# Ten seven-product quads per sweep in place of eight, the first weight sum of each made in DRAM by an accumulating DMA

## The chip, the cores and the metric

One NeuronCore of one Trainium2 chip runs the whole program. The metric is device time in microseconds (us) of one execution; the median of three runs of the kernel before is 1942.89 us.

The engines are named as the profile names them: PE multiplies matrices (PEld is its weight load, which overlaps), DVE is the vector engine, ACT the scalar engine, POOL is GpSimd, and SP issues most of the DMAs. Each engine runs its own list of instructions in order and waits on semaphores. The DMAs of SP, ACT and POOL are carried by the core's 16 DMA engines.

## The reference

Two layers on a sequence of 256 tokens with 2048 channels, in float32. Layer 0 mixes tokens with a convolution module, layer 1 with latent attention; each is followed by an MLP of width 8192.

```python
for layer in range(2):
    h = rms_norm(x, norm_mixer_g[layer])
    x = x + (conv_module(h, ...) if layer == 0 else mla(h, ...))
    h = rms_norm(x, norm_mlp_g[layer])
    x = x + jnp.square(jax.nn.relu(h @ mlp_w1[layer])) @ mlp_w2[layer]
return rms_norm(x, final_norm_g)
```

The convolution module multiplies by a 2048x4096 matrix (`conv_w_pw1`), gates, applies a causal depthwise convolution of width 31, normalizes, and multiplies by a 2048x2048 matrix.

## The kernel before

**Products in three parts.** Every float32 operand is split into a rounded part `hi` (ACT, one copy) and the rest `lo` (a subtraction, `lo = raw - hi`); a product is then three matmuls, hi by hi, lo by hi and hi by lo (`mm3`, L202 to L204). So each weight block costs a DMA into `raw` (three buffers), one pass of ACT and one pass of DVE or POOL (L169 and L173, or L431 and L432 in a quad), into six `hi` and six `lo` buffers of up to 128x1024.

**The convolution stage** runs over 16 chunks of 128 channels. The weights of one chunk come in two loads, and their four `lo` passes are made by POOL (L173 on POOL), which also multiplies the gate (L815) and adds a half sum (L872). DVE applies the taps of the depthwise convolution (L875), PE multiplies (L788).

**The MLP** takes the hidden width in two halves of 4096, so there are four halves in the program. Of each half, the up product makes eight groups `g` of 512 hidden channels (L645, L646; the activations are in `xt`, sixteen tiles of 128 channels), and squares and splits them (L663 to L673). The down product then makes two sweeps, each over 1024 output columns and all 32 k-tiles of the half, taken by twos: a **plain pair** is 2 k-tiles by 2 column blocks by 2 token blocks, 8 products or 24 matmuls of 512 columns; a **quad** reaches the same result with 7 products, 21 matmuls, from sums of weight blocks and sums of inputs (a Strassen scheme in Winograd's form). Groups 0, 2, 4 and 6 are `mixed` (eight quads per sweep), groups 1, 3, 5 and 7 plain (eight plain pairs). The weight sums of a quad are made by DVE in `raw` (L439, L440, L441), the input sums at the end of the up product of their group (`mixed_inputs`, L459 to L462). Each sweep holds all eight PSUM banks: four for the outputs and four for sums that `join` and `close` add in at the end; in the first half of a layer they are added to `xs` by accumulating DMAs that POOL issues (L512), 24 in the program.

**The order.** The program is written in one sequence, but a scheduler places each engine's instructions by its own estimate of when their inputs are ready; an instruction that waits for nothing can be put far ahead of where it is written. `MIXED`, `HEAD`, `TAIL` and `LAST_TAIL` set where quads stand among the plain pairs: before, a first sweep begins P P q q P q q (P a plain pair, q a quad).

Of the kernel before, what the change touches and what calls it, by code (L numbers as in the profile page):

```python
# [10 lines left out]
F32 = mybir.dt.float32  # L11
# [7 lines left out]
P = 128  # L19
# [23 lines left out]
LOOK = WB // 2 - 1  # L43
MIXED = {(0, 0): (0, 2, 4, 6), (0, 1): (0, 2, 4, 6), (1, 0): (0, 2, 4, 6), (1, 1): (0, 2, 4, 6)}
N_MIXED = 4
HEAD, TAIL, LAST_TAIL = (2, 1), 2, 3

# [31 lines left out]
def trunk_kernel(  # L79
# [31 lines left out]
    wpool = ctx.enter_context(tc.tile_pool(name="wpool", bufs=2))  # L111
    small = ctx.enter_context(tc.tile_pool(name="small", bufs=2))
    psum, psum_cx = {}, [ExitStack()]

# [235 lines left out]
    def open_xt(name):  # L350
        pool = right_pool(name, 1)
        xt[:] = [
            pool.tile([P, KC // NNB, 2 * S], F32R, name=nm("xt")) for _ in range(NNB)
        ]

    xhl = lambda k: xt[k // 4][:, k % 4, :]
    xh = lambda k: xhl(k)[:, :S]
# [65 lines left out]

    def mixed_weights(raw):

        def halves(src):
            hi = wpool.tile(list(src.shape), F32R, tag="hi", name=nm("hi"), bufs=WB)
            lo = wpool.tile(list(src.shape), F32R, tag="lo", name=nm("lo"), bufs=WB)  # L430
            nc.scalar.activation(hi, src, AF.Copy)  # L431
            nc.vector.tensor_tensor(lo, src, hi.bitcast(F32), op=ALU.subtract)  # L432
            return [(hi[:, i, :], lo[:, i, :]) for i in range(src.shape[1])]

        b11, b21 = halves(raw[:, :, :NB])
        (b22,) = halves(raw[:, 1:2, NB:])
        top = raw[:, 0, :].rearrange("p (c n) -> p c n", c=2)
        low = raw[:, 1, :].rearrange("p (c n) -> p c n", c=2)
        nc.vector.tensor_tensor(top, raw[:, :, NB:], top, op=ALU.subtract)  # L439
        nc.vector.tensor_tensor(low[:, 1, :], low[:, 1, :], top[:, 0, :], op=ALU.subtract)  # L440
        nc.vector.tensor_tensor(low[:, 0, :], low[:, 0, :], low[:, 1, :], op=ALU.subtract)  # L441
        t1, t3 = halves(top)
        t4, t2 = halves(low)
        return b11, b21, b22, t1, t2, t3, t4

    def mixed_inputs(v, fh, fl):

        def halves(src, at, n):  # L450
            hi, lo = fh[:, at : at + n, :], fl[:, at : at + n, :]
            nc.scalar.activation(hi, src, AF.Copy)
            nc.vector.tensor_tensor(lo, src, hi.bitcast(F32), op=ALU.subtract)

        a = v.rearrange("p k (t n) -> p (k t) n", t=T)
        a11, a21, a12, a22 = (a[:, i, :] for i in range(4))
        halves(a[:, 0:1, :], 0, 1)
        halves(a[:, 2:4, :], 1, 2)
        nc.vector.tensor_tensor(a22, a21, a22, op=ALU.add)  # L459
        nc.vector.tensor_tensor(a21, a11, a21, op=ALU.subtract)  # L460
        nc.vector.tensor_tensor(a11, a22, a11, op=ALU.subtract)
        nc.vector.tensor_tensor(a12, a12, a11, op=ALU.subtract)  # L462
        halves(a, 3, 4)

    class Sums:
# [13 lines left out]

        def mixed(self, w, k, fh, fl, end):  # L480

            b11, b21, b22, t1, t2, t3, t4 = mixed_weights(load([rows(w, k, 2, self.n * NB, 2 * NB)], 2))
            u1, u6, u7, u5 = self.u
            work = [
                (u1, 0, b11), (u5, 6, t1), (u7, 4, t3), (u6, 3, t2),
                (self.e[0][0], 1, b21), (self.e[0][1], 5, b22), (self.e[1][0], 2, t4),
            ]
            if self.begun:
                work = [work[i] for i in (0, 4, 5, 1, 2, 6, 3)]
            for ps, i, (wh, wl) in work:  # L490
                mm3(ps, fh[:, i, :], fl[:, i, :], wh, wl, self.first(ps), end and any(ps is u for u in self.u))
# [24 lines left out]
        def join(self, room):  # L516
# [6 lines left out]
            nc.vector.tensor_tensor(c, u7, b, op=ALU.add)  # L523
            nc.vector.tensor_tensor(d, u5, c, op=ALU.add)
            nc.vector.tensor_tensor(b, u5, b, op=ALU.add)
            for (t, n), o in (((1, 0), c), ((1, 1), d), ((0, 1), b)):
# [75 lines left out]
    def mlp(layer, ssq, next_gain, finish=None, before=None, between=None, beside=None, after_up=None):  # L602

        with ExitStack() as cx:
# [22 lines left out]
            for hf in range(HALVES):  # L627
                last = hf == HALVES - 1
                mixed = MIXED[layer, hf]
                plain = [g for g in range(ng) if g not in mixed]  # L630
                gs = {}
                for g in range(ng):
                    ps = [acc_tile() for _ in range(4)]
                    c0 = (hf * nkh + 4 * g) * P
                    for u in range(KC // 4):
# [3 lines left out]
                        for j in range(4):  # L639
                            k = 4 * u + j  # L640
                            wh, wl = wj(j)
                            for b in range(4):
# [3 lines left out]
                                nc.tensor.matmul(ps[b][:, :S], wl[:, bs], xh(k), start=False, stop=k == KC - 1)  # L646
                        step(6)
                    if hf == g == 0:
                        scales()
                    if beside is not None and g == 2:  # L650
                        beside(mp)
                        beside = None
                    if g in mixed or g in plain[len(plain) + len(mixed) - N_MIXED :]:
                        shape = [P, 2, 7, P] if g in mixed else [P, 4, S]
                        gs[g] = [mp.tile(shape, F32R, tag=f"s{c}", name=nm(f"s{c}"), bufs=N_MIXED) for c in "hl"]
                    else:
                        gs[g] = [mp.tile([P, 4, S], F32R, tag=f"g{c}", name=nm(f"g{c}"), bufs=ng - N_MIXED) for c in "hl"]
                    gh, gl = gs[g]
# [15 lines left out]
                nssq, add, prepare = residual_stage(last, next_gain)  # L674
                w, k_lo = mlp_w2[layer], hf * nkh
                at_kt = lambda i: lambda k, t: gs[k // 4][i][:, k % 4, t * P : (t + 1) * P]
                hi, lo = at_kt(0), at_kt(1)
                ms = [(g, b) for g in mixed for b in range(2)]
                due = []

                def mixed_quad(sums, i):
                    g, b = ms[i]
                    sums.mixed(w, k_lo + 4 * g + 2 * b, gs[g][0][:, b], gs[g][1][:, b], i == len(ms) - 1)

                split_end = last and finish is not None
                for n in range(0, NNB, 2):
# [5 lines left out]
                    if ends:  # L692
                        after_up()
                    for i, k in enumerate(ks[: -tail] if ends else ks):
                        upto = -(-len(ms) * (i - head + 1) // (len(ks) - head - tail + 1))
                        while at < min(upto, len(ms)):
                            mixed_quad(sums, at)
                            at += 1
                        if i == len(ks) - tail + 1:
                            sums.join(room)  # L700
# [22 lines left out]
    with ExitStack() as cx:  # L723
# [235 lines left out]
        with tc.manual_schedule():  # L959
# [85 lines left out]
            def part(ks, p):  # L1045
                return xt[ks[0] // 4][:, ks[0] % 4 : ks[0] % 4 + len(ks), p * S : (p + 1) * S]

# [744 lines left out]
    with ExitStack():  # L1792
        gfs = []

        def load_gf():
            gfs.append(right_pool("gf", 1).tile([P, D], F32, name="gf"))
            nc.scalar.dma_start(gfs[0], final_norm_g.rearrange("(a n) -> a n", a=1).partition_broadcast(P))
# [90 lines left out]
```

## Time and profile before

| what | value |
|---|---|
| runs | 1942.15, 1942.89, 1943.25 us; median 1942.89 |
| profiled execution | span 1940.9 us from first to last instruction; granted clock 0.998 |
| convolution stage, weights split on POOL | 12 to 197 us of the span |
| up products of the MLP | 300 to 478, 641 to 819, 1246 to 1424, 1587 to 1765 us |
| down products, two sweeps each | 478 to 641, 819 to 985, 1424 to 1587, 1765 to 1931 us |
| DMA | 373.93 MB, mean 193 GB/s |

The profile is of one execution, whose span is 1940.9 us, 2.0 us under the median of the runs. Busy time counts instructions that follow each other closely with their overlap, so an engine that never waits may show a little more than its window. In tables by stretches of time, the number in brackets behind a busy time is that of instructions. A wait is put down to what ended it.

### The profile page before, as it was taken

The numbers are of one execution on the slowest core, as the hardware profiler recorded it, in microseconds if no ns is written. First come the engines' busy times: TensorE is split into PE (matmuls) and PEld (weight loads), VectorE is DVE, ScalarE is ACT, GpSimd is POOL, SyncE is SP. The second block draws the span as 40 slices with busy tenths as digits, with TensorE's granted clock in tenths as the row PEclk, the third lists the DMA queues.
The fourth block names the chain that finished last, engine by engine and source line by source line (L and its number), as shares of the span: only waits on it lengthen the run. The fifth ranks groups of instructions, "written<-read, shape, count | busy, mean of one in ns | idle before, by whom it ended". The sixth has DMA issues, their size and how long they took to land. (4 is left out here: it accounts for less than half of the span.)

```text
span 1940.9 us, 28606 instructions
## 1 busy us (share of the span) xinstructions
PE 1920.0 (99%) x10799; PEld 1683.0 (87%) x10799; DVE 1604.5 (83%) x2490; ACT 1095.4 (56%) x1636; POOL 241.9 (12%) x196
## 2 busy tenths in 40 slices
PE   8999999999999999999999999999999999999997
PEld 8999888888888888888889998888888888888876
DVE  7999988877999667799976766877789986778998
ACT  5667755555565455455666565555555555555655
POOL 6999200000010000000002310000000010000000
PEclk9999999999999999999999999999999999999999
DMA  7766456555576866555665445466546786555654
GB/s 230 212 188 182 156 192 209 186 192 174 190 233 222 249 191 195 174 183 201 204 197 149 141 135 192 155 214 194 185 163 224 221 268 198 185 187 186 224 184 142
DMA packets 214571, 373.93 MB, mean 193 GB/s; under 512 B 15896, under 2 KB 90912, under 8 KB 214176
## 3 DMA queue, kind: packets, MB, share of 16 engines
q1 hardware_dynamic: 209648, 363.28, 58.1%
q0 software_dynamic: 3456, 6.29, 1.8%
q10 hardware_dynamic: 1328, 2.52, 0.4%
q8 instruction: 84, 1.38, 0.3%
q14 instruction: 55, 0.45, 0.1%
HBM read 363.68 MB, written 2.10 MB: 188 GB/s over the span
## 5 line engine op out<-in xcount | busy, mean ns | idle before, releaser
L173 DVE TENSOR_TENSOR lo<-raw,hi 128x1024 fp32r<-128x1024 f32 (+2 forms) x503 | 598.5, 1204 | 249.1 <-ACT hi L169 245.6
L169 ACT ACTIVATE hi<-raw 128x1024 fp32r<-128x1024 f32 (+1 forms) x568 | 578.8, 1038 | 357.8 <-PE acc L645 212.6
L645 PE MATMUL acc<-xt,hi 128*128 128x512 f32 x2048 | 710.5, 390 | 0.0
L646 PE MATMUL acc<-xt,lo 128*128 128x256 f32 x2048 | 577.5, 282 | 0.0
L645 PEld LDWEIGHTS acc<-xt,hi 128*128 128x128 f32 x2048 | 384.4, 188 | 80.6
L646 PEld LDWEIGHTS acc<-xt,lo 128*128 128x128 f32 x2048 | 387.1, 189 | 0.2
L431 ACT ACTIVATE hi<-raw 128x1024 fp32r<-128x1024 f32 (+1 forms) x256 | 235.6, 947 | 233.5 <-DVE raw L439 151.5
L432 DVE TENSOR_TENSOR lo<-raw,hi 128x1024 fp32r<-128x1024 f32 (+1 forms) x256 | 271.9, 1086 | 22.4 <-ACT hi L431 18.1
L204 PE MATMUL acc<-lo,sh 128*128 128x512 f32 x512 | 199.6, 390 | 1.9 <-DVE lo L432 1.9
L204 PE MATMUL acc<-lo,gh 128*128 128x512 f32 (+1 forms) x516 | 199.9, 388 | 0.8 <-DVE lo L173 0.8
L202 PE MATMUL acc<-hi,gh 128*128 128x512 f32 (+1 forms) x516 | 200.0, 388 | 0.0
L203 PE MATMUL acc<-hi,gl 128*128 128x512 f32 (+1 forms) x516 | 199.9, 387 | 0.0
L202 PE MATMUL acc<-hi,sh 128*128 128x512 f32 x512 | 199.6, 390 | 0.2 <-ACT hi L431 0.2
L788 PE MATMUL acc<-xt,hi 128*128 128x256 f32 x1024 | 180.1, 281 | 0.3 <-ACT b L1070 0.2
L203 PE MATMUL acc<-hi,sl 128*128 128x512 f32 x448 | 174.3, 389 | 0.0
L875 DVE SCALAR_TENSOR_TENSOR sum<-ub,w_dw,sum 128x256 f32<-128x256 f32 x409 | 164.2, 480 | 3.5 <-ACT sum L845 3.0
L173 POOL TENSOR_TENSOR lo<-raw,hi 128x1024 fp32r<-128x1024 f32 x65 | 155.1, 2412 | 17.3 <-ACT hi L169 17.3
L788 PEld LDWEIGHTS acc<-xt,hi 128*128 128x128 f32 x1024 | 154.6, 188 | 1.1 <-ACT xt L1054 0.6
L788 PE MATMUL acc<-xt,lo 128*128 128x256 f32 x512 | 139.2, 279 | 0.0
L512 POOL DMA_DIRECT2D xs<-v x24 | 21.1, 961 | 882.7 <-DVE lo L173 701.5
L204 PEld LDWEIGHTS acc<-lo,sh 128*128 128x128 f32 x512 | 96.1, 188 | 23.2 <-DVE lo L432 3.2
L204 PEld LDWEIGHTS acc<-lo,gh 128*128 128x128 f32 x516 | 96.8, 188 | 21.1 <-DVE lo L173 1.3
(309 smaller groups left out, 2568.2 us busy)
## 6 DMA issues: line engine op xcount, KB each, us to landing
raw<-in_mlp_w SPq DMA_DIRECT2D x256, 1024.0 KB, 5.4
raw<-in_conv_w_pw SPq DMA_DIRECT2D x62, 512.0 KB, 5.1
raw<-in_conv_w_pw SPq DMA_DIRECT2D x16, 1024.0 KB, 5.0
raw<-in_mla_w_o SPq DMA_DIRECT2D x16, 1024.0 KB, 5.4
raw<-in_mla_w_kv_up SPq DMA_DIRECT2D x8, 1024.0 KB, 5.4
xs<-v POOLq DMA_DIRECT2D x24, 256.0 KB, 7.6
raw<-in_mla_w_in SPq DMA_DIRECT2D x8, 576.0 KB, 3.8
raw<-in_mla_w_in SPq DMA_DIRECT2D x4, 1024.0 KB
```

The lines of the kernel that those rows point to most:

```text
L169: nc.scalar.activation(hi, raw[:, js, :], AF.Copy)
L173: eng.tensor_tensor(lo, raw, hi.bitcast(F32), op=ALU.subtract)
L202: nc.tensor.matmul(ps, sh, mh, start=start, stop=False)
L203: nc.tensor.matmul(ps, sl, mh, start=False, stop=False)
L204: nc.tensor.matmul(ps, sh, ml, start=False, stop=stop)
L431: nc.scalar.activation(hi, src, AF.Copy)
L432: nc.vector.tensor_tensor(lo, src, hi.bitcast(F32), op=ALU.subtract)
L512: nc.gpsimd.dma_start(x, o, accum_op=ALU.add)
L645: nc.tensor.matmul(ps[b], wh[:, bs], xhl(k), start=k == 0, stop=False)
L646: nc.tensor.matmul(ps[b][:, :S], wl[:, bs], xh(k), start=False, stop=k == KC - 1)
L788: nc.tensor.matmul(pss[c][b][:, :S], w[i][:, bs], (xh, xl)[j](k), start=k == i + j == 0, stop=end and k == k0 + nk - 1 and (i, j) == terms ...
L875: nc.vector.scalar_tensor_tensor(out=out, in0=ubs[c][:, w : w + S], scalar=tap(c, w), in1=base, op0=ALU.mult, op1=ALU.add)
```

## The change

1. Groups 0, 2, 4, 6 and 7 are mixed: ten quads and six plain pairs per sweep in place of eight and eight. A first sweep now begins P q q q P q q.
2. The inputs of group 7's quads are written into the last eight tiles of `xt`, which is kept in DRAM meanwhile (`spare`, 2 MB out and back in the first half of each layer).
3. The scheme's signs change so that the first weight sum, q1 = b12 + b11, is a pure sum. It is made in DRAM: SP copies b12 there (128x512, 256 KB) and POOL issues a DMA that adds b11 to it. There are 80 of them, 10 for each of 8 sweeps. In the code they stand in the up product, one for each weight load.
4. A quad's `raw` is then loaded by three DMAs (q1, then b21 and b22, then b11) in place of one, and DVE makes three sums of 128x512 where it made one of 128x1024 and two of 128x512. All quads take their products in the order in which the weights are made.
5. `gf` (the final norm's gain) is loaded into the MLP's pool.

```diff
-MIXED = {(0, 0): (0, 2, 4, 6), (0, 1): (0, 2, 4, 6), (1, 0): (0, 2, 4, 6), (1, 1): (0, 2, 4, 6)}
-HEAD, TAIL, LAST_TAIL = (2, 1), 2, 3
+MIXED = (0, 2, 4, 6, 7)
+HEAD, TAIL, LAST_TAIL = (1, 1), 2, 3
@@ mixed_weights
+        raw = wpool.tile([P, 4, NB], F32, tag="raw", name=nm("raw"), bufs=3)
+        nc.sync.dma_start(raw[:, 3, :], q1)
+        nc.sync.dma_start(raw[:, 1:3, :], low.rearrange("p (c n) -> p c n", c=2))
+        nc.sync.dma_start(raw[:, 0, :], top[:, :NB])
-        b11, b21 = halves(raw[:, :, :NB])
-        (b22,) = halves(raw[:, 1:2, NB:])
-        nc.vector.tensor_tensor(top, raw[:, :, NB:], top, op=ALU.subtract)
-        nc.vector.tensor_tensor(low[:, 1, :], low[:, 1, :], top[:, 0, :], op=ALU.subtract)
-        nc.vector.tensor_tensor(low[:, 0, :], low[:, 0, :], low[:, 1, :], op=ALU.subtract)
-        t1, t3 = halves(top)
-        t4, t2 = halves(low)
+        b22, q1 = halves(2, 4)
+        nc.vector.tensor_tensor(raw[:, 3, :], raw[:, 3, :], raw[:, 2, :], op=ALU.add)
+        b11, b21 = halves(0, 2)
+        nc.vector.tensor_tensor(raw[:, 0, :], raw[:, 3, :], raw[:, 0, :], op=ALU.subtract)
+        nc.vector.tensor_tensor(raw[:, 1, :], raw[:, 3, :], raw[:, 1, :], op=ALU.add)
+        (q2,) = halves(3, 4)
+        q3, q4 = halves(0, 2)
@@ mlp, up product, behind each weight load
+                        while half_done:
+                            q1, src = half_done.pop(0)
+                            nc.gpsimd.dma_start(q1, src, accum_op=ALU.add)
+                        if sums_due:
+                            q1 = first_sums[key] = dram.tile([P, NB], F32, name=nm("q1"))
+                            nc.sync.dma_start(q1, row[:, NB:])
+                            half_done.append((q1, row[:, :NB]))
...
+                    if not last and g == 1:
+                        nc.sync.dma_start(spare, xt[2].bitcast(F32))
...
+                    if g == IN_XT:
+                        room_x = xt[2].rearrange("p k n -> p (k n)")[:, XT_PAD : XT_PAD + 4 * 7 * P]
```

**Where it moves instructions.** Neither the copies nor the accumulating DMAs wait for anything that the program computes, and the scheduler has put all 80 of both into the convolution stage. POOL there, one chunk before, from the gate's product on:

```order
L815 TENSOR_TENSOR ub_7_122<-vb_180_1587,sg_179_1585 128x256
L173 TENSOR_TENSOR lo_184_1593<-raw_159_1417,hi_183_1592 128x1024
L872 TENSOR_TENSOR half_171_1470<-half_171_1470,tp_168_1435 128x256
L173 TENSOR_TENSOR lo_189_1604<-raw_159_1417,hi_188_1603 128x1024
L173 TENSOR_TENSOR lo_193_1689<-raw_172_1472,hi_192_1688 128x1024
L173 TENSOR_TENSOR lo_195_1693<-raw_172_1472,hi_194_1692 128x1024
```

POOL now, in the same chunk (L846, L175 and L903 are what L815, L173 and L872 were; L660 is the accumulating DMA into a `q1`):

```order
L846 TENSOR_TENSOR ub_6_123<-vb_179_1588,sg_178_1586 128x256
L660 DMA q1_2124_13586<-in_mlp_w2 128x512
L175 TENSOR_TENSOR lo_183_1594<-raw_158_1418,hi_182_1593 128x1024
L660 DMA q1_2138_13671<-in_mlp_w2 128x512
L660 DMA q1_2144_13716<-in_mlp_w2 128x512
L660 DMA q1_2150_13761<-in_mlp_w2 128x512
L660 DMA q1_2156_13806<-in_mlp_w2 128x512
L903 TENSOR_TENSOR half_170_1471<-half_170_1471,tp_167_1436 128x256
L660 DMA q1_2170_13875<-in_mlp_w2 128x512
L660 DMA q1_2176_13920<-in_mlp_w2 128x512
L175 TENSOR_TENSOR lo_188_1605<-raw_158_1418,hi_187_1604 128x1024
L175 TENSOR_TENSOR lo_192_1690<-raw_171_1473,hi_191_1689 128x1024
```

Most chunks now hold 8 or 9 accumulating DMAs, and all 80 stand between POOL's 2nd and 47th pass of 65 over weights; each waits for its copy to land, and from the ninth on for the accumulating DMA eight places before it.

SP in the same stage, before (the loads of the chunks' weights):

```order
L159 DMA raw_209_1805<-in_conv_w_pw1 128x8x128 x2
L159 DMA raw_215_1915<-in_conv_w_pw1 128x8x128 x2
L159 DMA raw_228_1970<-in_conv_w_pw1 128x8x128 x2
L159 DMA raw_233_2083<-in_conv_w_pw1 128x8x128 x2
L159 DMA raw_246_2138<-in_conv_w_pw1 128x8x128 x2
```

SP now (L666 is the copy into a `q1`):

```order
L161 DMA raw_208_1806<-in_conv_w_pw1 128x8x128 x2
L161 DMA raw_214_1916<-in_conv_w_pw1 128x8x128 x2
L666 DMA q1_2634_16607<-in_mlp_w2 128x512
L666 DMA q1_2648_16692<-in_mlp_w2 128x512
L666 DMA q1_2654_16737<-in_mlp_w2 128x512
L666 DMA q1_2660_16782<-in_mlp_w2 128x512
L666 DMA q1_2666_16827<-in_mlp_w2 128x512
L666 DMA q1_2680_16896<-in_mlp_w2 128x512
L666 DMA q1_2686_16941<-in_mlp_w2 128x512
L666 DMA q1_2692_16986<-in_mlp_w2 128x512
L666 DMA q1_2698_17031<-in_mlp_w2 128x512
L161 DMA raw_227_1971<-in_conv_w_pw1 128x8x128 x2
```

A batch of up to nine copies now stands between two chunks' weight loads, and SP reaches it only when POOL has freed the `raw` buffer of the load ahead.

DVE in a sweep, one quad before:

```order
L432 TENSOR_TENSOR lo_747_5694<-raw_745_5691,hi_746_5693 128x1024
L432 TENSOR_TENSOR lo_749_5698<-raw_745_5691,hi_748_5697 128x512
L439 TENSOR_TENSOR raw_745_5691<-raw_745_5691 128x1024
L440 TENSOR_TENSOR raw_745_5691<-raw_745_5691 128x512
L441 TENSOR_TENSOR raw_745_5691<-raw_745_5691 128x512
L432 TENSOR_TENSOR lo_751_5705<-raw_745_5691,hi_750_5704 128x1024
L432 TENSOR_TENSOR lo_753_5709<-raw_745_5691,hi_752_5708 128x1024
```

DVE now, one quad:

```order
L442 TENSOR_TENSOR lo_746_5667<-raw_744_5662,hi_745_5666 128x1024
L442 TENSOR_TENSOR lo_748_5672<-raw_744_5662,hi_747_5671 128x1024
L446 TENSOR_TENSOR raw_744_5662<-raw_744_5662 128x512
L448 TENSOR_TENSOR raw_744_5662<-raw_744_5662 128x512
L449 TENSOR_TENSOR raw_744_5662<-raw_744_5662 128x512
L442 TENSOR_TENSOR lo_750_5678<-raw_744_5662,hi_749_5677 128x512
L442 TENSOR_TENSOR lo_752_5682<-raw_744_5662,hi_751_5681 128x1024
```

The last `lo`, of 128x1024, needs ACT's copy of what L448 and L449 wrote; between L449 and it stands one `lo` of 128x512, where before one of 128x1024 stood between L441 and the last.

More of the change, by code (lines that the diff above doesn't have):

```diff
@@ L43 @@
 LOOK = WB // 2 - 1
[L44 to L46 removed]
+MIXED = (0, 2, 4, 6, 7)
+IN_XT = 7
+XT_PAD = 56
+HEAD, TAIL, LAST_TAIL = (1, 1), 2, 3
 SIDE = {KC - 3: 2, KC - 2: 4}
@@ L351, in open_xt, with xrows @@
         pool = right_pool(name, 1)
[L352 to L356, printed above, removed]
+        xt[:] = [pool.tile([P, n, 2 * S], F32R, name=nm("xt")) for n in (KC // 4, KC // 4, KC // 2)]
+    def xrows(k, n):
+        i = min(k // 4, 2)
+        return xt[i][:, k - 4 * i : k - 4 * i + n, :]
+    xhl = lambda k: xrows(k, 1)[:, 0, :]
     xh = lambda k: xhl(k)[:, :S]
@@ L698, in mlp @@
                             at += 1
+                        if not last and n == NNB - 2 and i == len(ks) // 2:
+                            nc.sync.dma_start(xt[2].bitcast(F32), spare)
                         if i == len(ks) - tail + 1:
```

69 lines of the change are left out of this document (40 added, 29 removed).

## Prediction

> **What bounds the kernel now.** I read the page's first two parts, then a table by stretches of time, since the stages differ.
>
> ```profile
> PE 1920.0 (99%) x10799; PEld 1683.0 (87%) x10799; DVE 1604.5 (83%) x2490; ACT 1095.4 (56%) x1636; POOL 241.9 (12%) x196
> POOL 6999200000010000000002310000000010000000
> ```
>
> ```profile
> core 0: us, PE busy (x) PEld busy (x) DVE busy (x) ACT busy (x) POOL busy (x), PEclk, DMA share, GB/s
> 15.00:147.00 132.00, 131.94 (x1131) 131.70 (x1130) 126.92 (x320) 84.24 (x145) 124.47 (x67) 1.00 0.69 202
> 300.00:478.00 178.00, 178.00 (x1029) 157.78 (x1028) 139.38 (x242) 95.53 (x140) 0.00 (x0) 1.00 0.60 191
> 478.00:641.00 163.00, 163.00 (x722) 135.01 (x721) 153.28 (x164) 92.90 (x105) 8.85 (x10) 1.00 0.67 215
> 818.70:985.00 166.30, 165.54 (x738) 136.49 (x736) 160.86 (x188) 95.35 (x118) 0.25 (x2) 1.00 0.58 192
> ```
>
> PE is busy everywhere, so fewer matmuls are fewer microseconds as long as nobody else becomes late. Two places leave little room. In the convolution stage POOL, which is 12% busy over the whole, is busy 124.5 of the 132.0 us from 15 to 147, and the 16 DMA engines 69%. In the sweeps (300 to 478 us is an up product, 478 to 641 the pair of sweeps of a first half, 819 to 985 that of a last half) DVE is busy 153.3 of 163.0 and 160.9 of 166.3 us.
>
> **Part 1: seven products more often.** Two plain pairs per sweep become quads, which takes 2 x 3 matmuls of 512 columns from each of 8 sweeps: 48. PE issues 722 in 163.0 us, 0.226 us each: **-10.8 us** where PE stays the bound, 160.3 us for a pair of sweeps.
>
> **Part 2: 80 sums in DRAM, issued inside the convolution stage.** What they cost hangs on where they stand, and the built order puts them between the 2nd and the 47th of POOL's 65 passes over the convolution's weights; by the gate products beside them that is the stretch from 15 to about 147 us. POOL's timeline of one chunk:
>
> ```profile
> start us, us, engine line op out<-in xcount [idle before <-releaser]
> 96.37 0.74 POOL L815 TENSOR_TENSOR ub<-vb,sg 128x256 f32<-128x256 f32 x1 [0.18 <-ACT vb L814]
> 97.37 2.43 POOL L173 TENSOR_TENSOR lo<-raw,hi 128x1024 fp32r<-128x1024 f32 x1 [0.26 <-ACT hi L169]
> 99.75 0.75 POOL L872 TENSOR_TENSOR half<-half,tp 128x256 f32<-128x256 f32 x1
> 100.44 7.14 POOL L173 TENSOR_TENSOR lo<-raw,hi 128x1024 fp32r<-128x1024 f32 x3
> 107.86 0.74 POOL L815 TENSOR_TENSOR ub<-vb,sg 128x256 f32<-128x256 f32 x1 [0.27 <-ACT vb L814]
> ```
>
> A chunk takes 11.49 us (96.37 to 107.86) and POOL idles 0.53 of them. Everything behind an accumulating DMA on POOL waits for it: the `lo` passes, so PE's products by `lo`, and the gate's product, so DVE's taps. The same kind of DMA, with `xs` in place of a DRAM tile, is in the trace:
>
> ```profile
> L512 POOL DMA_DIRECT2D xs<-v x24: 850/870/1222, 547.0 to 1592.6; - x24
> ...
> DMA to landing us min/median/max: 5.7/7.6/10.1
> ```
>
> On POOL, at the median: 80 x 0.87 = 69.6 us, of which the stretch's idle 7.5 us (132.0 - 124.5) can take in some: **+62 us at least**; at the longest, 1.22 us, 97.8 - 7.5 = +90. That is the price if POOL alone is late.
>
> The transfers cost the DMA engines as well. Two rows of what the queues took, first from 15 to 147 us, then in the first pair of sweeps, which shows plain rows of MLP weights (q1) beside accumulation (q0); the columns are packets, MB, and the share of 16 engines:
>
> ```profile
> q1 hardware_dynamic: 50717, 26.50, 68.6%
> ```
>
> ```profile
> q1 hardware_dynamic: 9488, 32.81, 59.8%
> q0 software_dynamic: 1155, 2.10, 7.0%
> ```
>
> The stretch's own loads are 0.686 x 132 = 90.6 us of all 16 engines. In the sweeps (163 us) q1 moves 1 MB in 0.598 x 163 / 32.81 = 2.97 us, so a copy of 256 KB (0.262 MB) takes 0.78 us; q0 took 0.070 x 163 / 8 = 1.42 us for each of its eight accumulations of 256 KB. No row shows a transfer from DRAM to DRAM. From below I take these two prices, since the bytes are the same. From above I double the accumulation, since it must also read its target from DRAM: into SBUF it already costs 1.8 times a copy. I take the lower ones, from the rows nearest in kind. 80 x (0.78 + 1.42) = 176 us, and 90.6 + 176 = 267 us of work for a stretch of 132: +135 if all 16 engines never idle. The last eight accumulations, 8 x 1.42 = 11 us, may still be under way when POOL has gone on, so **+123 us**; at the doubled price +226. The 62 us of POOL lie within this, not on top: it is the same time seen from another engine.
>
> SP is passed too. Its loads, with KB each and the median us to landing:
>
> ```profile
> raw<-in_mlp_w SPq DMA_DIRECT2D x256, 1024.0 KB, 5.4
> raw<-in_conv_w_pw SPq DMA_DIRECT2D x62, 512.0 KB, 5.1
> ```
>
> Now each batch of copies stands ahead of the next weight loads (at most 9 x 0.78 = 7 us of DMA time that those loads come later), and it is reached only when POOL has freed a buffer, so POOL's accumulations wait for copies issued 8 to 10 instructions earlier. At a landing time near 5 us that is hidden behind those instructions (about 8 us); as the DMA engines fill up it is part of the 123.
>
> The Trainium skill prices a POOL-issued DMA differently: in "DMA: Bandwidth & Descriptors", section "Anatomy of one DMA — SWDGE (gpsimd) path", it gives about 2.0 us of fixed time plus bytes / 436e9. By that the moving part of 256 KB is 0.60 us, 80 sums are 80 x 1.2 = 96 us, the DMA engines have 187 us of work there, less than POOL's 124.5 + 69.6 = 194, and POOL sets the end. By the skill the sum would be that of rival A, by the trace that of part 2. The trace disagrees (1.42 us against 0.60), so I hold to the trace.
>
> **Part 3: the quads' weights on DVE.**
>
> ```profile
> 499.88 1.22 DVE L439 TENSOR_TENSOR raw<-raw 128x1024 f32<-128x1024 f32 x1
> ...
> 503.76 2.96 DVE L432 TENSOR_TENSOR lo<-raw,hi 128x1024 fp32r<-128x1024 f32 x3
> 506.64 1.22 DVE L439 TENSOR_TENSOR raw<-raw 128x1024 f32<-128x1024 f32 x1
> 507.89 0.69 DVE L440 TENSOR_TENSOR raw<-raw 128x512 f32<-128x512 f32 x1
> 508.62 0.69 DVE L441 TENSOR_TENSOR raw<-raw 128x512 f32<-128x512 f32 x1
> 509.23 2.52 DVE L432 TENSOR_TENSOR lo<-raw,hi 128x1024 fp32r<-128x1024 f32 x2
> 511.67 2.35 DVE L173 TENSOR_TENSOR lo<-raw,hi 128x1024 fp32r<-128x1024 f32 x2
> ```
>
> ```profile
> 509.43 1.06 ACT L431 ACTIVATE hi<-raw 128x1024 fp32r<-128x1024 f32 x1 [0.39 <-DVE raw L441]
> ```
>
> Two quads that follow each other take DVE 6.76 us each (499.88 to 506.64), a plain pair 2.3 us. A pass of 128x1024 starts 1.15 us behind the one before it, one of 128x512 0.61 us (508.62 to 509.23), or 0.73 us if it needs that one's result (507.89 to 508.62). Now: two passes 2.30, L446 0.73, L448 0.61, and then the catch: ACT can copy the result only when L449 has ended (0.69), begins 0.12 us later (L441 ended at 509.31, ACT began at 509.43), takes 1.06, and DVE goes on 0.03 us later; the one short `lo` hides in that 1.90 us. With the last pass, 1.15, a quad is 6.69 us. So the change saves DVE instructions but only 0.07 us of its time per quad. A pair of sweeps: 20 x 6.69 + 12 x 2.3 = 161.4, against 16 x 6.76 + 16 x 2.3 = 145.0: +16.4 us. The sums of group 7's inputs come on top, at the start of the first sweep:
>
> ```profile
> L453 DVE TENSOR_TENSOR sl<-v,sh 128x256 fp32r<-128x256 f32 x8 | 3.3, 417 | 0.0
> L453 DVE TENSOR_TENSOR sl<-v,sh 128x128 fp32r<-128x128 f32 x8 | 2.3, 287 | 0.1
> L460 DVE TENSOR_TENSOR v<-v 128x128 f32<-128x128 f32 x8 | 2.3, 286 | 0.1
> ```
>
> 2 x (0.42 + 0.29 + 4 x 0.29) = 3.7 us. A first half's pair then holds DVE for 153.3 + 16.4 + 3.7 = 173.4 us, where PE needs 160.3: DVE is the bound, **+10.4 us**. In a last half 160.9 + 20.1 = 181.0 against 166.3, +14.7, of which I take 12, because the two plain pairs at each sweep's end give DVE 10.9 us of PE's time to catch up. Together 2 x 10.4 + 2 x 12 = **+45 us**. The bounds are -11 (the 1.90 us are filled somehow, and PE stays the bound) and +59 (14.7 four times). P q q q in place of P P q q at the start makes DVE late at the third quad already.
>
> **Costed at nothing:** the three loads for one per quad (the same 1 MB; three `raw` buffers give a load two quads of DVE time, 13 us, against a landing near 5); the 2 MB out and back of `xt`, which PE needs only half a stage later; ACT's copies (92.9 of 163 us busy); `gf`, loaded a sweep ahead. The up products keep their own loads and get no sums.
>
> **Sum.** 1940.9 + 123 + 45 = 2109; the profiled span lies 2.0 us under the median, so **2111 us**.
>
> **Rivals.**
> A. POOL alone is late in the convolution stage and the DMA engines keep up. For it: the accumulation's 1.42 us is a share in packets' time, and packets of different queues may overlap. Against: 267 us of work in a stretch that POOL alone would make 194. +62 to +90, with the sweeps 1940.9 + 76 + 45 + 2 = 2064.
> B. Accumulating in DRAM costs twice as much. For it: one more read per element; no row excludes it. 1940.9 + 226 + 45 + 2 = 2214.
> C. The sweeps stay PE's. For it: 94% busy before, PE never waited there. Against: the 1.90 us chain. 1940.9 + 123 - 11 + 2 = 2055.
> D. Faster: PE stays the bound in all stages, 1942.9 - 10.8 = 1932. In the sweeps that is C; for the stage with the sums it takes POOL to be free of them: it has 7.5 us for 80, so it decides at 0.09 us each, against a shortest row of 0.85. That the kernel doesn't do what it says is part of the forecast: the sums don't lie under the up products.
>
> **Chances.** Forecast 0.50, A 0.20, B 0.11, C 0.14, D 0.04, anything else 0.01. The range takes in C and A down to POOL's +62 with PE-bound sweeps (1940.9 + 62 - 11 + 2 = 1994, so 1995) and B (2214, to 2225). 0.2%, 3.9 us, is about what a measurement of this kernel can tell from no change: faster 0.04, same 0.01, slower 0.95. Slower cases hold nearly all, so no second range is needed.
>
> **What the profile after would show.** POOL near full, with L660, and PE idle behind L175 on POOL, and the first up product starting some 123 us later than at 300 us; a DMA share over 0.9 in the stretch (A: under 0.9 with POOL full, and 62 to 90 us later; B: over 0.9, and 226 us later). In the pairs of sweeps 173 us with PE waiting for DVE L442 and DVE for ACT L441 about 0.6 us per quad (C: 160 us, and no such wait). The up products unchanged at 178 us. Wrong would be the forecast if L660 took POOL far less than 0.85 us, or if its landing, not POOL or bandwidth, set the pace: eight may be under way, 80 / 8 x 10.1 us = 101 us at the longest landing, less than the stretch has.

## The result and the profile after

The changed kernel takes 2158.68 us, median of five runs (2154.45 to 2160.82), against 1942.83 for the kernel before in runs beside it: ratio 1.1111, 95% interval 1.1097 to 1.1124. The profiled execution spans 2156.7 us. The forecast was 2111 us. These parts of the page answer to the first two that the prediction shows; POOL's row and PE's granted clock (PEclk) and the DMA share are by 40 slices of the span:

```profile
PE 1975.4 (92%) x10751; PEld 1695.4 (79%) x10751; DVE 1633.7 (76%) x2618; ACT 1122.4 (52%) x1684; POOL 306.9 (14%) x276
...
POOL 5666567000000000000000051000000000000000
PEclk8877789999999999999999999999999999999999
DMA  9989994656655768664655644566564768654654
```

PE has 48 matmuls fewer and is no longer busy throughout. The first six slices, some 320 us, are another picture than the rest: PE's clock is granted in part only and the DMA engines are full.

The stages by the starts of PE's first and last matmul in each, worked out from the two traces (us). The first row, called the convolution stage from here on, runs to 264.7 us of the span before and to 429.2 us now, so it takes in the first part of the second pointwise product (the one by the 2048x2048 matrix):

| stage | before | after | difference | forecast |
|---|---|---|---|---|
| convolution stage, with the first part of the second pointwise product | 260.6 | 425.0 | +164.4 | +123 |
| rest of the second pointwise product | 35.3 | 35.3 | 0 | 0 |
| up products 1 and 3 (first halves) | 177.6, 177.6 | 181.6, 185.3 | +4.0, +7.7 | 0 |
| up products 2 and 4 (last halves) | 177.4, 177.4 | 178.0, 178.5 | +0.6, +1.1 | 0 |
| pairs of sweeps, first halves | 163.0, 163.0 | 172.2, 171.9 | +9.2, +8.9 | +10.4 each |
| pairs of sweeps, last halves | 166.2, 166.7 | 174.6, 175.9 | +8.4, +9.2 | +12 each |
| attention | 259.4 | 261.5 | +2.1 | 0 |

The differences add up to 215.6; the spans differ by 215.8. The table leaves out the pauses between stages: the one ahead of the attention is 1.5 us shorter now, the stretch behind the last matmul 1.6 us longer. Three quarters of the loss lie in the convolution stage, before any of the 80 sums is used. A table by stretches of time, in the columns of the prediction's table (the stretch with the sums; the first up product; a first half's pair of sweeps; a last half's):

```profile
20.00:310.00 290.00, 158.50 (x1118) 155.16 (x1116) 122.87 (x308) 80.47 (x138) 185.79 (x145) 0.76 0.98 231
464.00:646.00 182.00, 179.85 (x1028) 158.94 (x1027) 140.55 (x244) 94.37 (x139) 0.00 (x0) 0.99 0.60 195
646.00:819.00 173.00, 168.67 (x713) 130.81 (x712) 155.87 (x190) 97.91 (x115) 8.79 (x10) 1.00 0.66 209
997.00:1172.00 175.00, 170.26 (x728) 132.47 (x726) 164.84 (x214) 103.42 (x131) 0.25 (x2) 1.00 0.55 179
```

The work that took 132 us now takes 290. POOL is busy 185.8 of them, 64%, so it is not the engine that is full; the DMA engines are, at 0.98. What the queues took from 20 to 310 us (packets, MB, share of 16 engines), and how long a copy (SPq) and an accumulation (POOLq) took from issue to landing over the whole span:

```profile
q1 hardware_dynamic: 59876, 46.25, 55.4%
q0 software_dynamic: 11312, 20.62, 41.9%
```

```profile
q<-in_mlp_w SPq DMA_DIRECT2D x80, 256.0 KB, 11.9
q<-in_mlp_w POOLq DMA_DIRECT2D x80, 256.0 KB, 8.6
```

An accumulation into DRAM took 0.419 x 290 / 80 = 1.52 us of all 16 engines (1.42 into SBUF before); 20.62 of the 20.97 MB fall in the window, so this is some 2% low. If the stage's own loads still took 90.6 us, a copy took (0.554 x 290 - 90.6) / 80 = 0.88 us, an estimate.

Waits in the same stretch (the longest of PEld, PE and DVE, and two of POOL's), and two of POOL's groups:

```profile
PEld acc L819 <- POOL lo L175: 133.9, 15, 18.1
PE acc L819 <- POOL lo L175: 130.7, 14, 17.9
DVE sum L906 <- ACT sum L876: 89.2, 11, 20.8
POOL q L660 <- issue: 59.6, 27, 6.3
POOL q L660 <- DMA q<-in_mlp_w: 43.9, 13, 7.8
```

```profile
L175 POOL TENSOR_TENSOR lo<-raw,hi 128x1024 fp32r<-128x1024 f32 x45 | 119.4, 2820 | 0.7 <-ACT hi L171 0.7
L660 POOL DMA_DIRECT2D q<-in_mlp_w x80 | 74.8, 1055 | 105.6 <-issue 59.6 <-DMA q<-in_mlp_w 43.9 <-PE acc L819 2.0
```

PE waits for POOL's `lo` passes, 130.7 us in 14 pieces; before, PE had no wait there at all and was busy 131.9 of 132 us. That row alone would name POOL the culprit. The second fence says otherwise: POOL stands idle 105.6 us ahead of L660, waiting for copies to land and for something that the profile does not name ("issue"). The `lo` passes are late because they stand behind accumulating DMAs that wait for the DMA engines.

In the sweeps, the kernel before from 478 to 641 us, then the changed kernel from 646 to 819 us:

```profile
DVE lo L432 <- ACT hi L431: 3.8, 3, 1.4
```

```profile
DVE lo L442 <- ACT hi L441: 9.7, 16, 0.6
PEld acc L206 <- DVE lo L442: 8.5, 16, 1.0
PEld acc L204 <- ACT hi L441: 6.4, 15, 0.9
```

DVE now waits 16 times, 0.6 us each, for ACT's last copy of a quad, and PE's weight loads, which waited for nobody from 478 to 641 us before, wait for DVE and for ACT.

### The profile page after: what moved, and what is told of

Its sections match the earlier page's. It is cut to its first block, busy times and chain, and to the rows that moved or that the text cites. A ratio compares the mean times of both kernels' runs of the same rounds, so it can differ in the third digit from the quotient of the medians.

```text
span 2156.7 us, 29317 instructions
## 1 busy us (share of the span) xinstructions
PE 1975.4 (92%) x10751; PEld 1695.4 (79%) x10751; DVE 1633.7 (76%) x2618; ACT 1122.4 (52%) x1684; POOL 306.9 (14%) x276
## 4 chain that ended last, share of the span: by engine, by line
PE 51%; issue 6%; DVE 5%; ACT 2%; DMA 1%; POOL 0%; DVEq 0%; ACTq 0%; POOLq 0%
PE acc L655 15%; PE acc L204 8%; PE acc L656 8%; PE acc L205 8%; PE acc L206 8%; DVE lo L442 2%; ACT hi L441 1%; DMA xs<-v 1%; DVE lo L175 1%; DMA raw<-in_mlp_w 1%; DVE raw L449 1%; DVE raw L446 0%; ACT hi L171 0%; DVE cq L325 0%; PE acc L1666 0%
## 5 line engine op out<-in xcount | busy, mean ns | idle before, releaser
L175 DVE TENSOR_TENSOR lo<-raw,hi 128x1024 fp32r<-128x1024 f32 (+2 forms) x471 | 559.7, 1203 | 232.2 <-ACT hi L171 226.8
L171 ACT ACTIVATE hi<-raw 128x1024 fp32r<-128x1024 f32 (+2 forms) x536 | 544.0, 1037 | 367.5 <-PE acc L655 182.8
L441 ACT ACTIVATE hi<-raw 128x1024 fp32r<-128x1024 f32 (+1 forms) x320 | 291.7, 946 | 255.8 <-DVE raw L446 147.3
L656 PEld LDWEIGHTS acc<-xt,lo 128*128 128x128 f32 x2048 | 389.1, 190 | 1.9 <-DVE lo L175 1.8
L442 DVE TENSOR_TENSOR lo<-raw,hi 128x1024 fp32r<-128x1024 f32 (+1 forms) x320 | 338.0, 1087 | 45.1 <-ACT hi L441 45.0
L819 PEld LDWEIGHTS acc<-xt,lo 128*128 128x128 f32 x512 | 106.7, 213 | 137.8 <-POOL lo L175 137.8
L819 PE MATMUL acc<-xt,hi 128*128 128x256 f32 x1024 | 202.3, 302 | 0.3 <-ACT xt L1085 0.2
L175 POOL TENSOR_TENSOR lo<-raw,hi 128x1024 fp32r<-128x1024 f32 x65 | 167.3, 2705 | 14.2 <-ACT hi L171 14.2
L204 PE MATMUL acc<-hi,gh 128*128 128x512 f32 (+1 forms) x388 | 151.2, 390 | 0.0
L205 PE MATMUL acc<-hi,gl 128*128 128x512 f32 (+1 forms) x388 | 150.1, 388 | 0.0
L206 PE MATMUL acc<-lo,gh 128*128 128x512 f32 (+1 forms) x388 | 144.1, 387 | 0.0
L204 PEld LDWEIGHTS acc<-hi,sh 128*128 128x128 f32 x512 | 96.0, 188 | 46.7 <-ACT hi L441 28.6
```

The costliest lines, as they stand in the source:

```text
L171: nc.scalar.activation(hi, raw[:, js, :], AF.Copy)
L175: eng.tensor_tensor(lo, raw, hi.bitcast(F32), op=ALU.subtract)
L204: nc.tensor.matmul(ps, sh, mh, start=start, stop=False)
L205: nc.tensor.matmul(ps, sl, mh, start=False, stop=False)
L206: nc.tensor.matmul(ps, sh, ml, start=False, stop=stop)
L819: nc.tensor.matmul(pss[c][b][:, :S], w[i][:, bs], (xh, xl)[j](k), start=k == i + j == 0, stop=end and k == k0 + nk - 1 and (i, j) == terms ...
```

## The experiments

Each ran beside the kernel before (1942.4 to 1942.6 us). They are in the order of what they isolate.

**The sums by themselves.** The kernel before, with this in its up-product loop:

```diff
+ while half_done:
+     q1, src = half_done.pop(0)
+     nc.gpsimd.dma_start(q1, src, accum_op=ALU.add)
+ if sums_due:
+     ...
+     nc.sync.dma_start(q1, row[:, NB:])
+     half_done.append((q1, row[:, :NB]))
```

> The kernel before, unchanged in its arithmetic, with the 80 DRAM sums of the change beside it: the same 80 copies on SP's queue and 80 accumulating DMAs on POOL's, written at the same places; nothing reads them. Theory (the DMA engines are the bound of the convolution stage once the sums stand there): nearly all of the stage's +164 us comes with the sums alone, so 2095 to 2115 us, the first up product some 160 us later than in the kernel before, the pairs of down sweeps still at 163 and 166.5 us. Rival (the sums are mostly hidden, and it is the changed layout of buffers or the new quads that delay the stage): under 1980 us.

2110.92 us, ratio 1.0863 (1.0845 to 1.0882): +168.6. The stage takes 429.7 us, and every stage behind it is that of the kernel before (177.6, 163.0, 177.4, 165.9 us in the first layer). The loss in the convolution stage is the sums, not the new layout.

**The change without the sums.** The quads load the right half of the top rows straight from the weight:

```diff
- first_sums[n, at], i == len(ms) - 1
+ w[(k_lo + 4*g + 2*b) * P : (k_lo + 4*g + 2*b + 1) * P, (n + 1) * NB : (n + 2) * NB], i == len(ms) - 1
```

> The changed kernel without the DRAM sums: the quads load the right half of the top rows straight from the weight, so the second term of the first sum is left out; copies and accumulates are gone, all else stays. Theory: the convolution stage is back at its 260 us, so 2158.7 - 164 = 1995 us (1988 to 2002); the four pairs of down sweeps stay at 172 to 176 us and the first and third up products at 181 and 185 us. Rival (the quads' loads from the DRAM tiles are what makes the sweeps longer, through their wait for the accumulates or their place in memory): sweeps back at 160 to 163 us, 1945 to 1960 us.

1993.99 us (1.0250 to 1.0281 times before), as expected: the convolution stage is back at 260.6 us, the pairs of sweeps stay at 172.9 to 176.0. So the change has two losses that add: 164.7 us by the sums, 51.6 us in the MLP itself.

**What in the sums is dear: bytes or issues.** First the accumulations alone were made narrow:

```diff
- nc.gpsimd.dma_start(q1, src, accum_op=ALU.add)
+ nc.gpsimd.dma_start(q1[:, :64], src[:, :64], accum_op=ALU.add)
```

> The changed kernel with each of the 80 accumulating DMAs cut to the first 64 of its 512 columns (7/8 of the second terms are left out); the copies, the number of DMAs, their place and their issues on POOL are unchanged. Theory (bytes through the DMA engines): an accumulate costs 0.2 to 0.5 us of the 16 engines in place of 1.54, so 80 to 107 us of engine work goes; the stretch with the sums shrinks from 290 to about 185 to 210 us and the time falls to 2050 to 2080 us. Rival A (POOL's issues of 0.84 us each delay its lo passes, whatever the DMAs carry): no change, 2150 to 2160 us.

2112.42 us: only 46 us less, where my theory wanted 80 to 107. The rows from 20 to 270 us:

```profile
20.00:270.00 250.00, 163.02 (x1103) 158.68 (x1102) 123.37 (x310) 80.22 (x139) 187.19 (x146) 0.80 0.78 196
```

```profile
q1 hardware_dynamic: 59859, 46.21, 64.9%
q0 software_dynamic: 11520, 2.63, 12.5%
```

An accumulation now takes 0.125 x 250 / 80 = 0.39 us, so 90 us of DMA work did go; but at a DMA share of 0.78 the engines are no longer the limit, and something else close behind them is. POOL is not full either: it is busy 187 of the 250 us, 75%. To see it by itself, copies and accumulations both at 64 columns, beside the kernel without sums:

```diff
- q1 = first_sums[key] = dram.tile([P, NB], F32, name=nm("q1"))
+ q1 = first_sums[key] = dram.tile([P, 64], F32, name=nm("q1"))
- nc.sync.dma_start(q1, row[:, NB:])
- half_done.append((q1, row[:, :NB]))
+ nc.sync.dma_start(q1, row[:, NB : NB + 64])
+ half_done.append((q1, row[:, :64]))
```

> The kernel without DRAM sums (the second term of the first sum left out, 1994.0 us) with 80 small sums beside it that nothing reads: a copy of 64 columns on SP's queue and an accumulating DMA of 64 columns on POOL's, at the places of the full ones. Cutting the accumulates alone to 64 columns had brought only 46 us of 165, so three theories stand. DMA engines alone: at 0.39 us of the 16 engines for each small DMA the stretch of 132 us has some 90 + 62 us of DMA work: 2005 to 2025 us. POOL's issues: 80 x 0.81 us less the 7.5 us that POOL had idle: 2045 to 2060 us. The loop of waits (a lo pass on POOL stands behind accumulates, these wait for copies, the copies stand on SP's queue behind loads, and these wait for a buffer that a lo pass frees): it does not shrink with the bytes, 2080 to 2115 us.

2083.77 us: +89.8 over the kernel without sums, with hardly a byte moved. POOL and the DMA share from 20 to 236 us, and POOL's waits from 15 to 240:

```profile
20.00:236.00 216.00, 156.09 (x1096) 153.37 (x1097) 121.67 (x307) 79.18 (x138) 189.22 (x147) 0.83 0.61 141
```

```profile
POOL q L660 <- issue: 19.2, 15, 2.3
POOL q L660 <- DMA q<-in_mlp_w: 8.9, 3, 7.2
```

The time falls into the range of the loop of waits, but the rows give most of it to POOL's work: POOL is busy 189 of 216 us (124.5 of 132 before), which is 65 us more or 0.81 us for each of 80 issues, and it waits 28 us. The 0.81 us is a net figure: POOL's records of an issue and of the pass behind it overlap, and the passes over weights lengthen to 2.86 us from 2.41. The second limit, then, is POOL's issues lengthened by its waits, and it costs 90 us even where the bytes are gone. The converse, the bytes with half the issues, beside the kernel before:

```diff
- q1 = dram.tile([P, NB], F32, name=nm("q1"))
- row = w2[k * P : (k + 1) * P, n * NB : (n + 2) * NB]
+ q1 = dram.tile([P, 2 * NB], F32, name=nm("q1"))
+ row, other = (w2[(k + j) * P : (k + j + 1) * P, n * NB : (n + 2) * NB] for j in range(2))
+ ...
```

> The kernel before with unread DRAM sums beside it, as in the kernel with the sums alone (2110.9 us), but 40 of 512 KB (1024 columns of two rows of blocks) in place of 80 of 256 KB: the same bytes through the DMA engines with half the issues on SP and on POOL. The run with small sums had shown that 80 issues cost 90 us even without the bytes; this one keeps the bytes. Theory (the stage has two limits close together and the larger one counts, with full bytes the DMA engines): no fall beyond the better use of 4 KB rows, 2085 to 2115 us, DMA share still above 0.95 in the stretch. Rival (POOL's issues and its waits for the copies are the limit with full bytes too): half of the 90 us goes, 2050 to 2070 us.

2093.15 us: 17.8 less than with 80 sums, not the 40 or more of the rival.

```profile
20.00:290.00 270.00, 150.98 (x1101) 148.41 (x1100) 123.36 (x310) 80.72 (x139) 153.51 (x106) 0.78 0.98 243
```

POOL is busy 57% of the stretch and the DMA share is 0.98 again. With full bytes the DMA engines are the limit. What the 17.8 us are, half the issues or the longer rows, this run does not separate.

**The sums elsewhere.** The same 80 sums, held back in groups 1 to 5 of each up product by a one-element DMA from the activations of the group before; copies and accumulations on POOL's queue:

```diff
+ if g > 0:
+     mark = gs[g - 1][0]
+     ...
+     for key in batch:
+         first_sums[key] = dram.tile([P, NB], F32, name=nm("q1"))
+         nc.gpsimd.dma_start(first_sums[key][0:1, 0:1], mark)
+     for part in range(2):
+         for n, i in batch:
+             ...
+             if part == 0:
+                 nc.gpsimd.dma_start(first_sums[n, i], src)
+             else:
+                 nc.gpsimd.dma_start(first_sums[n, i], src, accum_op=ALU.add)
```

> The changed kernel with all 80 sums made later: in every up product the groups 1 to 5 issue four sums each, copies and accumulates all on POOL's queue, each held back by one small DMA that reads the activations of the group before. Arithmetic unchanged. Theory (the sums cost time only where they stand: POOL is idle in the up products and their DMA share of 0.6 leaves some 70 us of the 178 for 20 x 2.3 = 46 us): the convolution stage is back at 260 us and the time is that of the kernel without sums, 1994 us, plus at most 10: 1990 to 2004 us. Rival (the sums lengthen the up products through the DMA engines that the weight loads use, as they did the convolution stage): 4 x 10 us or more on top, 2035 us and above.

1991.99 us (1.0239 to 1.0269): the time of the kernel without sums, so 166.7 us came back with the move. It changed two things, the place and, for the copies, the queue (POOL's in place of SP's); no run separates them. The first up product, with 20 sums under it:

```profile
300.00:480.00 180.00, 177.92 (x1027) 157.46 (x1026) 139.97 (x244) 94.84 (x139) 38.08 (x60) 1.00 0.85 255
```

```profile
q0 software_dynamic: 5120, 10.49, 27.3%
```

The 40 DMAs (with 20 of one element) take 0.273 x 180 / 20 = 2.46 us per sum of the 16 engines, nearly the price in the convolution stage (0.88 + 1.52 = 2.40). There they met a share of 0.69 in 132 us, here 0.60 in 178 us with a quarter of the sums: 0.85, and PE stays at 177.9 of 180.

**The chain in the quad.** Without sums, the last pair's copy and subtraction in two:

```diff
- q3, q4 = halves(0, 2)
+ hi, lo = (wpool.tile([P, 2, NB], F32R, tag=c, name=nm(c), bufs=WB) for c in ("hi", "lo"))
+ for i in range(2):
+     nc.scalar.activation(hi[:, i, :], raw[:, i, :], AF.Copy)
+ for i in range(2):
+     nc.vector.tensor_tensor(lo[:, i, :], raw[:, i, :], hi[:, i, :].bitcast(F32), op=ALU.subtract)
+ ...
```

> As the kernel without DRAM sums (the second term of the first sum left out), and in each quad the ACT copy and the DVE subtraction of the last pair (q3 and q4, 1024 columns each) are cut in two of 512, so that DVE need not wait for an ACT copy of 1024 columns at the quad's end. Theory (the chain DVE last sum - ACT copy - DVE subtraction leaves DVE idle 0.6 us per quad and makes it the bound): 80 quads get about 0.5 us each back less one more start of a DVE instruction, 25 to 35 us in all where PE has the next limit, so the pairs fall to 162 to 167 us and the time to 1960 to 1972 us. Rival (DVE is the bound by its work, or the three loads per quad are): within 5 us of the kernel without the cut.

1980.91 us: 13.1 less, about half of what I expected. The stall was real, but it was not all: the pairs come to 169.8 to 173.3 us. From 480 to 650 us:

```profile
480.00:650.00 170.00, 167.07 (x710) 130.50 (x708) 156.38 (x209) 99.58 (x133) 8.80 (x10) 1.00 0.67 209
```

DVE is still busy 156 of 170 us. Whether its work is what holds the sweeps, one sum less per quad tries, on this kernel with `xt` copied out in four:

```diff
- nc.vector.tensor_tensor(raw[:, 3, :], raw[:, 3, :], raw[:, 2, :], op=ALU.add)
```

> The kernel without DRAM sums, with the last pair cut in two and xt copied out in four (the second terms of the first and of the second weight sum left out): one DVE sum of 512 columns less per quad, 20 x 0.685 = 13.7 us per pair of sweeps; with that sum it would take some 1975 us. Theory (DVE's work bounds the sweeps, PE only their least): the pairs fall from 170 to 161 to 164 us, the time to 1940 to 1952 us. Rival (the three loads per quad or the order of the products hold PE): 1968 us or more.

1948.01 us (1.0015 to 1.0037), inside the theory's range for the time. The pairs fall to 164.6 to 165.5 us, a little less than it wanted:

```profile
478.00:643.00 165.00, 162.80 (x708) 131.55 (x707) 146.40 (x191) 98.17 (x133) 8.53 (x10) 1.00 0.70 217
```

DVE's busy time fell by 10 us and the pair by 5, so DVE's part in the quads does hold the sweeps. Whether by the amount of its work or by its place in the chain is not separated: the sum that is left out also stood ahead of L448 and L449, and DVE was never full (156 of 170 us, now 146 of 165). This kernel, which makes neither of the first two sums on the chip's engines or in DRAM, still isn't faster than the kernel before. It lies 5.4 us behind, with a third up product that is 4.6 us longer than before (182.2 us for 177.6), so with 48 matmuls less the sweeps take about as long as before. PE's 160.3 us were not reached; what holds the last 5 us per pair was not separated.

**The copy of `xt`.** Without sums, the 2 MB in four parts behind groups 1 to 4:

```diff
- if not last and g == 1:
-     ...
-     nc.sync.dma_start(spare, xt[2].bitcast(F32))
+ if not last and 1 <= g <= 4:
+     ...
+     part = slice((g - 1) * KC // 8, g * KC // 8)
+     nc.sync.dma_start(spare[:, part, :], xt[2][:, part, :].bitcast(F32))
```

> The kernel without DRAM sums (the second term of the first sum left out, 1994.0 us), with the 2 MB of xt copied out in four DMAs of 512 KB behind groups 1, 2, 3 and 4 in place of one of 2048 KB behind group 1. Theory (the one large copy holds up the weight load behind it for 5.3 to 7.7 us, and the first and third up products take 181.6 and 185.3 us for 177.6): both up products back at 178 to 179 us, 1982 to 1988 us. Rival (the two up products are longer for their DVE or buffers): within 2 us of 1994 us.

1988.14 us, 5.9 less, 0.1 us above the theory's range and far from the rival's. The first up product is back at 177.6 us, the third at 179.5 (in later runs with the same edit at 180.0 to 182.2), so the third is mended in part only. What the one large copy did, in the changed kernel's timeline of SP's queue, ACT and PE:

```profile
476.94 0.35 SPq L672 DMA_DIRECT2D spare<-xt  x1
```

```profile
487.77 1.06 ACT L171 ACTIVATE hi<-raw 128x1024 fp32r<-128x1024 f32 x1 [5.28 <-DMA raw<-in_mlp_w]
```

```profile
490.47 0.50 PE L655 MATMUL acc<-xt,hi 128*128 128x512 f32 x1 [2.15 <-DVE v L691]
```

ACT waits 5.28 us for the weight load issued behind it and passes that on to DVE, and PE stands 2.15 us; in the third up product ACT waits 7.7 us and PE 4.6.

**Mends together.** Late sums, the split chain, the `xt` copy in four, and besides, in `Sums.plain`, every second `lo` of a plain pair on POOL:

```diff
- at_j = split(load([rows(w, k, 2, self.n * NB, 2 * NB)], 2), nc.vector)
+ raw = load([rows(w, k, 2, self.n * NB, 2 * NB)], 2)
+ parts = [split_half(raw, h, (nc.vector, nc.gpsimd)[h]) for h in range(2)]
+ at_j = lambda j: [a[:, 0, :] for a in parts[j]]
```

> All four together, arithmetic unchanged: sums made late under the up products, the last pair's ACT copy and DVE subtraction cut in two of 512 columns, xt copied out in four, and in the down sweeps every second lo pass of the plain pairs of rows on POOL in place of DVE (12 of 24 per pair of sweeps, 1.22 us each, 14.6 us of DVE's 156). Theory (the sweeps are held by DVE: 156 us of work and some 13 us of waits against 160.3 us of PE): the pairs of sweeps fall to 160 to 163 us, and the time to 1928 to 1945 us. Rival (POOL's slower passes of 2.4 to 2.8 us come late and PE waits for them, or slow DVE down): 1960 us or more.

1989.66 us, a miss: the pairs of sweeps take 174.1 to 176.3 us, more than without POOL's passes. DVE's long passes in the kernel with the split chain, and in this one:

```profile
L442 DVE TENSOR_TENSOR lo<-raw,hi 128x1024 fp32r<-128x1024 f32 x38 | 45.8, 1221 | 3.4 <-ACT hi L441 3.4
```

```profile
L442 DVE TENSOR_TENSOR lo<-raw,hi 128x1024 fp32r<-128x1024 f32 x38 | 55.4, 1473 | 4.5 <-ACT hi L441 4.5
```

```profile
479.00:654.00 175.00, 169.71 (x714) 130.76 (x713) 157.15 (x200) 99.55 (x134) 36.04 (x21) 1.00 0.65 205
```

Ten passes left DVE, and its busy time stayed at 157 us, because the passes that stayed became longer: 38 in quads at 1.47 us in place of 1.22. The Trainium skill has this in "SBUF — State Buffer", section "Who interferes with whom": a DVE instruction with two inputs in SBUF contends with a GpSimd instruction that reads SBUF, over a shared pair of ports that the page calls an exclusive lock. The trace agrees in kind. The same without POOL's passes (the edit above taken back):

> The three mends that each took time away, together, arithmetic unchanged: sums under the up products on POOL's queue (1992.0 us by itself), the last pair's copy and subtraction in two (-13.1 us on the kernel without sums), xt copied out in four (-5.9 us). Theory (they act in different places): 1992.0 - 13.1 - 5.9 = 1973 us, 1968 to 1978. Rival (the sums meet the xt copies on the DMA engines, or the split's gain needs the cover that the sums take): 1982 us or more.

1969.82 us (1.0127 to 1.0157): 1992.0 - 13.1 - 5.9 = 1973.0, so the three add up, and a little more, and POOL's passes alone had cost 19.8 us. And with the first sweep's quads starting earlier:

```diff
- HEAD, TAIL, LAST_TAIL = (1, 1), 2, 3
+ HEAD, TAIL, LAST_TAIL = (0, 1), 2, 3
```

> As the kernel with the three mends, but in each half's first sweep the quads begin before the first plain pair of rows in place of behind it, so that they stand two by two between the plain pairs. Theory (a quad takes DVE 6.4 us and PE 4.8, a plain pair DVE 2.4 and PE 5.4: where ten quads stand with only three plain pairs among them DVE is the bound, though over the pair of sweeps it is not): 2 to 5 us less in each of the four first sweeps, 8 to 20 us in all, 1953 to 1965 us. Rival (the order makes no difference, or the first quads come before the up product's last inputs are ready): 1971 us or more.

1967.71 us (1.0109 to 1.0143). The intervals of the two overlap; the theory of crowded quads wanted 8 to 20 us and is not borne out. No version tried beats the kernel before.

## Why the prediction was right, and where it was off

The sign and the main mechanism held; the time came out 47.6 us over the forecast. By its own steps:

*Part 1* held in its count (10751 matmuls for 10799) and gave nothing: PE waits for DVE and ACT in every pair of sweeps.

*Part 2* named the place and the limit. The sums lie in the convolution stage, the DMA share there is 0.98, and moving them gives the time back. One sign failed: I expected POOL near full, and it is busy 64% of the stretch. Its size was too small, +123 for +164.4. The copy costs 0.88 us and not 0.78, the accumulation 1.52 and not 1.42: 80 x 0.20 = 16 us. The 11 us taken off for the last eight accumulations did not come off: L660 is issued until 309 us and PE's pace returns with it. At 0.98 in place of 1.00 the engines lost another 6 us. That is 33 of the 41 us; of the other 8 some 6 lie outside the 290 us of the stretch, and they were not traced. The bound from above, an accumulation of double price (rival B), is excluded: 1.52 is 1.07 times 1.42.

*Rival A* fell as a forecast, but its mechanism is there: POOL's issues cost 90 us when the bytes are taken away (I had +62 to +90). That this meets my upper figure is luck: I had reached 90 with the longest issue, 1.22 us, and the run reaches it with 0.81 us and 28 us of waits. Where I was wrong is in treating it as something wholly inside the DMA engines' time. Taking 90 us of DMA work away brings 46 us, and POOL's issues with their waits hold the rest. That POOL would set the end, an estimate from the formula of the Trainium skill's page "DMA: Bandwidth & Descriptors", section "Anatomy of one DMA — SWDGE (gpsimd) path", does not hold at full size: the trace has 1.52 us for an accumulation where the formula has 0.60 us for its bytes, and POOL is busy 64% of the stretch.

*Part 3* held in mechanism: DVE waits 0.6 us per quad for ACT's last copy, PE waits for DVE, first halves' pairs 172.2 and 171.9 us (forecast 173.4). That the size came so close is in part luck: the sum had DVE taken up for all of it, and the rows have DVE busy 155.9 us and waiting 9.7 us for ACT, 165.6 together. The last halves' pairs were over-priced, +8.4 and +9.2 for +12: the +14.7 of the sum, cut to 12 by judgement, should have been cut further. All sweeps together +35.7 for +45. The split chain showed that the stall is 13 us of it; a DVE sum less per quad took most of the rest away, by its work or by its place in the chain. *Rival C* and *rival D* fell: without any sums and with the chain mended the first pair of sweeps is still 170 us.

*Costed at nothing* was the step that failed outright. The three loads per quad, ACT's copies and `gf` showed no cost. The 2 MB out of `xt` did: +4.0 and +7.7 us in the first and third up products. I asked only when PE needs that data again, not what stands behind the copy on SP's queue. With the attention's +2.1 us, 1.5 of which the shorter pause ahead of it takes back, and +1.7 in the last halves' up products, not traced, that is 15.5 us not in the sum. 41.4 + 15.5 - 9.3 = 47.6, which is the miss.

## What to carry to other kernels

Work that waits for nothing is issued where a scheduler finds an idle slot on its own queue, and the price is set there by whoever the work fills first. Here POOL stood nearer its limit (busy 94% of the stretch, the DMA engines 69%), yet the sums brought 192 us of DMA work against some 65 us of POOL's, and the DMA engines filled first. The same 80 sums cost 165 us in the convolution stage and nothing under the up products. Read an engine's late instruction together with what stands ahead of it on its queue: PE waited for POOL, POOL for DMA. And when one limit is lifted by 90 us, look first for the second one close behind, since only the gap between them comes back, here 46 us.

## What the runs showed that I had not expected

An accumulating DMA of 256 KB from DRAM into DRAM costs 1.52 us of the 16 engines, hardly more than into SBUF (1.42); a plain copy from DRAM to DRAM about 0.88. Cut to 32 KB an accumulation still costs 0.39 us of the engines, and POOL some 0.81 us to issue.

PE's granted clock fell to 0.76 in the stretch, where PE is busy in pieces for 55% of the time. "TensorE: Matmul & The Clock Gate", section "What's actually happening", in the Trainium skill tells of a gate that halves the clock after an idle window of about 3.4 us; with PE's waits of up to 18 us the trace agrees. The clock is not likely to have set the time here: PE's busy time in the stretch rose from 131.9 to 158.5 us inside 290, and of POOL's 105.6 us of waits ahead of L660 only 2.0 were for PE.
